# Hybrid encoder layer on one core: first loads on ScalarE's queue, weight sums issued behind attention rows, six tail residuals on TensorE

## The chip, the cores and the metric

The kernel runs on one core of one Trainium2 chip. The time is device microseconds of a whole execution, the median of several; lower is better. The core has five engines with a queue of instructions each, which a reader meets below under the names of the profile: PE (TensorE, matrix products), DVE (VectorE), ACT (ScalarE), POOL (GpSimd) and SP (SyncE, which here only issues DMAs). Every engine works through its own instructions in order. DMAs are issued by SP, ACT or POOL.

## The reference

One layer: a mixer (multi-scale causal pooling beside stick-breaking attention, gated and merged) and a squared-ReLU MLP, each between RMSNorms. 1024 tokens, width 1024, eight heads of 64, MLP width 4096, all in float32.

```python
h = rmsnorm(x, g_pre_mix)
proj = einsum('bsd,de->bse', h, w_in)            # [u_pool | q | k | v]
y_pool = multiscale_pool(u_pool, w_pool_mix, pool_scale) @ w_br_pool
o_sb = stick_breaking_attention(q, k, v)         # query blocks of 128, strictly causal
y_sb = o_sb @ w_br_sb
gates = sigmoid(h @ w_gate + b_gate)
merged = gates[..., :D] * y_pool + gates[..., D:] * y_sb
x = x + rmsnorm(merged @ w_out, g_post_mix)
h2 = rmsnorm(x, g_pre_mlp)
ff = square(relu(h2 @ w_up)) @ w_down
x = x + rmsnorm(ff, g_post_mlp)
```

## The kernel before

Everything is kept transposed: 128 channels on the partitions, tokens along the free axis, in two halves `h` of 512 tokens. To keep float32 precision, an operand is split into a rounded part `hi` (a copy on ACT) and a rest `lo` (a subtraction on DVE), and each product is three matmuls, hi·hi, lo·hi and hi·lo (`mm3`, L115 to L117). The MLP uses a seven-product scheme in place of eight block products, which is why sums of blocks of `w_down` are needed.

The order of instructions on each engine is set by a list scheduler when the kernel is built: code order gives the priority, `issue_after(i)` holds an instruction behind another, and whatever the scheduler takes to be ready may be moved ahead into an idle place of its engine's queue. On the chip a queue is then worked off strictly in that order.

Stages and names that matter here:

- `phase_in`: loads `x` and the weights `wraw` of the first projection `u` in pieces, splits them into `whi`/`wlo` (L295, L296) and `x` into `hT_hi`/`hT_lo` (L325, L326), and takes squares for the norm (L332, L334). `vt` holds all small vectors, `gn` is made of it. Nine matmuls on zeros (`idle`, L313) run before the first data is there.
- `phase_attention`: for each of 8 heads, eight rows of scores in the order 7 to 0 (`att_scores`: products `z`, sigmoids `F` and `T` on ACT, a mask on `T` by POOL's AFFINE_SELECT at L567, a scan and a product on DVE). Then `att_steps` transposes `T` on PE (`at`), splits it into `ahi`/`alo` and multiplies with `v` into `o` (L615). In one step of each group, POOL fills a part of `ahi` and `alo` with zeros (MEMSET, L596 and L597), and the product `o` of that step needs it. Gates (`dg`, `job_gate`) and the next head's q, k and v fill PE's queue between. A gate's result `gs` goes to DRAM as `gscr` by a POOL DMA (L521).
- `weight_sums`: a generator of 32 POOL DMAs in eight groups of four, each 1 MB from DRAM to DRAM (`wscr`). A sum starts as a plain copy (L1058) and gets a second block by an accumulating DMA (L1056). With `s1, s2, s3, s4 = self.wscr`, the groups are s3, s1 (copies), s3, s1 (accumulate), s2 from s3 (copy), s2 (accumulate), s4 from s2 (copy), s4 (accumulate). Before the change `job_gate` takes one step after each of the 32 `gscr` DMAs.
- `phase_post`: splits the attention output `oT` into `oh`, `ol` (L732, L733), multiplies with `w_br`, loads the gates back (`gate`), merges; then the output projection.
- `down`, `norm`, `last_tokens`: the last product is made for two quarters of 256 tokens; the last quarter's norm `r`, scaling (L1243), residual and output DMAs are the end of the program. Four of eight residuals there are added by PE with an identity matrix (`sums_pe`, L1233 and L1248) and copied out by ACT (L1249), the others by DVE (L1252).

Of the kernel before, what the change touches and what calls it, by code (L numbers as in the profile page):

```python
# [52 lines left out]
class Block:  # L53
# [118 lines left out]
    def build(self):  # L172
# [48 lines left out]
        nc.scalar.preload_act_table_set(TABLES)  # L221
# [29 lines left out]
    def phase_in(self):  # L251
# [24 lines left out]

        for g in range(3):
            load_w(nc.gpsimd, g, 0, 256)
        load(0, 0, 1)
        nc.sync.dma_start(self.vt, self.vec)  # L280
        nc.vector.tensor_scalar(out=self.gn, in0=self.vt[:, 0:32], scalar1=-0.5, scalar2=None, op0=ALU.mult)
        load(0, 1, 1)
        load_w(nc.sync, 0, 256, 512)
        load(0, 2, 1)
        load_w(nc.sync, 1, 256, 512)
        load_w(nc.sync, 2, 256, 512)
        load(0, 3, 1)
        load_w(nc.sync, 0, 512, 1024)
        load(0, 4, 2)
        load_w(nc.sync, 1, 512, 1024)  # L290
        load_w(nc.sync, 2, 512, 1024)
        load(0, 6, 2)
        for a, b in ((0, 256), (256, 512), (512, 1024)):
            for raw, hi, lo in us:
                nc.scalar.copy(hi[:, a:b], raw[:, a:b])  # L295
                nc.vector.tensor_sub(lo[:, a:b], raw[:, a:b], hi[:, a:b].bitcast(F32))  # L296
# [15 lines left out]
        for _ in range(9):  # L312
            nc.tensor.matmul(idle, zero[:, :P], zero, start=True, stop=True)  # L313
# [3 lines left out]
        for h in range(2):  # L317
            hi = self.big.tile([P, NK, H], F32R, name=f"hT_hi{h}", tag=f"big_hi{h}")
            lo = self.big.tile([P, NK, H], F32R, name=f"hT_lo{h}", tag=f"big_lo{h}")
            self.hT.append((hi, lo))  # L320
            acc = pa.tile([P, H], F32, name="acc", bufs=2)
            accs.append(acc)
            for k in range(NK):
                g = self.gn[:, k : k + 1]
                nc.scalar.activation(hi[:, k, :], xs[h][:, k, :], AF.Copy, scale=g)  # L325
                nc.vector.scalar_tensor_tensor(  # L326
                    out=lo[:, k, :], in0=xs[h][:, k, :], scalar=g, in1=hi[:, k, :].bitcast(F32),
                    op0=ALU.mult, op1=ALU.subtract,
                )
            for k in range(NK):  # L330
                sq = pa.tile([P, H], F32, name="sq", bufs=3) if k else acc
                nc.scalar.activation(sq, xs[h][:, k, :], AF.Square)  # L332
                if k:
                    nc.vector.tensor_add(acc, acc, sq)  # L334
# [179 lines left out]
    def job_gate(self, i, h):  # L514
        nc = self.nc
        d = self.dps.tile([P, H], F32, name="dg", tag="d")
        yield from self.dense_steps(d, self.weights(("g", i)), self.hT[h])
        s = self.sp.tile([P, H], F32, name="gs", tag="gs", bufs=2)
        nc.vector.tensor_mul(s, d, self.rb[h])
        self.after = nc.scalar.activation(s, s, AF.Sigmoid, bias=self.vt[:, V_BG + i : V_BG + i + 1])  # L520
        out = nc.gpsimd.dma_start(self.gscr[i][:, h * H : h * H + H], s)  # L521
        with self.tc.issue_after(out.ins):
            next(self.wsums)
# [16 lines left out]
    def att_scores(self, h, i):  # L540
# [13 lines left out]
        for c in range((w - 1) // H * H, -1, -H):  # L554
            n = min(H, w - c)
            top = c + n == w
# [9 lines left out]
            if top:  # L566
                nc.gpsimd.affine_select(  # L567
                    out=tl[:, w - P : w], in_=tl[:, w - P : w], pattern=[[-1, P]], compare_op=ALU.is_gt, fill=0.0,
                    base=0, channel_multiplier=1,
                )  # L570
# [74 lines left out]
    def phase_attention(self):  # L645
# [11 lines left out]
        for h in range(8):  # L657
# [9 lines left out]
            for n_row, i in enumerate(ROWS):  # L667
# [3 lines left out]
                self.pump(w_in * share[n_row])  # L671
                if h == 0 and n_row < 4:
# [50 lines left out]
    def phase_post(self):  # L723
# [3 lines left out]
        self.banks = 1  # L727
        oh, ol = [], []
        for p in range(4):
            oh.append(pp.tile([P, 1024], F32R, name=f"oh{p}"))  # L730
            ol.append(pp.tile([P, 1024], F32R, name=f"ol{p}"))
            nc.scalar.copy(oh[p], self.oT[p])  # L732
            nc.vector.tensor_sub(ol[p], self.oT[p], oh[p].bitcast(F32))  # L733
# [15 lines left out]
        def gated(e, b, ds):  # L749
# [18 lines left out]
        for e in range(8):  # L768
# [21 lines left out]
        for h in range(2):  # L790
# [270 lines left out]
    def down(self):  # L1061
# [152 lines left out]
        def norm(h, x1, gap, c=slice(0, H), behind=(None,), last_part=False):  # L1214
# [14 lines left out]
            n_pe = 4 if last_part else 0  # L1229
# [5 lines left out]
            for e in range(8):  # L1235
# [7 lines left out]
                nc.vector.scalar_tensor_tensor(  # L1243
                    out=t, in0=t, scalar=self.gn[:, V_POST_MLP + e : V_POST_MLP + e + 1], in1=r,
                    op0=ALU.mult, op1=ALU.mult,
                )
# [6 lines left out]
                (nc.sync if h == 1 or e % 2 or behind[0] else nc.scalar).dma_start(self.out[h, e][:, c], t)  # L1253

        def last_tokens(c, ops, side):

            n = c.stop - c.start
            squares = []
            for e in range(4):
# [10 lines left out]
                nc.scalar.activation(sq, f, AF.Square)  # L1270
                if e > 1:
# [91 lines left out]
```

## Time and profile before

| | |
|---|---|
| median of 3 runs | 1279.74 us (1278.86 to 1281.45) |
| profiled execution | 1278.63 us, of which the span of the profile is 1276.9 us |
| mean granted PE clock in it | 0.999 |
| PE busy | 1265.7 us, 99% |
| DVE, ACT, POOL busy | 925.7 us (72%), 611.0 us (48%), 172.1 us (13%) |
| DMA queues | 143.64 MB issued by SP, 88.49 MB by POOL |

Times inside the profile count from the start of the span. The timeline gives start, duration, engine, line and operation, and in brackets how long the engine was idle before it and what ended that. For DMAs the duration in the timeline is the issue; the time to landing is in the list of DMA issues. POOL's DMAs are the `wscr`, `gscr`, `gate`, `ascr` and `xscr` traffic.

### The profile page before, as it was taken

To read this page: it belongs to the slowest core of one execution; us is meant where nothing else is said; L and a number is where in the kernel's file an instruction comes from. 1 tells how busy PE (TensorE), PEld (TensorE's weight loads), DVE (VectorE), ACT (ScalarE), POOL (GpSimd) and SP (SyncE) were. 2 spreads that over 40 slices of the span, in tenths; PEclk is the share of its full clock that TensorE was granted. 3 is DMA by queue.
4 is the path that set the end of the run, shared out by engine and by line. 5 is a ranking of instruction groups with operands and counts; after the bars stand their busy time and mean duration, and the time that the engine had idled before them with its cause. 6 is when DMAs were issued, how large, how long until landed. Compare 5 with 4: busy or idle time off the path is not lost.

```text
span 1276.9 us, 16588 instructions
## 1 busy us (share of the span) xinstructions
PE 1265.7 (99%) x6035; PEld 1056.1 (83%) x6035; DVE 925.7 (72%) x1317; ACT 611.0 (48%) x1012; POOL 172.1 (13%) x314
## 2 busy tenths in 40 slices
PE   9999999999999999999999999999999999999997
PEld 6898888889888887888878888888888888888887
DVE  8787688787878737551777979877785655776975
ACT  8235455555555533132456646455454433344452
POOL 1002213211213230000101002211120000001000
PEclk9999999999999999999999999999999999999999
DMA  6254637742757997451529578655569546547651
GB/s 226 66 165 153 210 90 181 147 106 53 185 157 197 248 229 234 142 195 33 179 79 307 181 245 283 216 191 205 177 238 345 194 153 224 191 176 242 200 212 66
DMA packets 75745, 233.70 MB, mean 183 GB/s; under 512 B 8624, under 2 KB 11184, under 8 KB 73488
## 3 DMA queue, kind: packets, MB, share of 16 engines
q1 hardware_dynamic: 47936, 143.64, 34.4%
q0 software_dynamic: 27152, 88.49, 23.1%
q8 instruction: 47, 0.77, 0.2%
q10 hardware_dynamic: 576, 0.52, 0.1%
q14 instruction: 34, 0.28, 0.1%
HBM read 178.10 MB, written 83.89 MB: 205 GB/s over the span
## 4 chain that ended last, share of the span: by engine, by line
PE 91%; DVE 4%; issue 2%; ACT 1%; DMA 1%; POOL 0%; SPq 0%; DVEq 0%; ACTq 0%; POOLq 0%
PE d L116 20%; PE d L117 20%; PE d L115 20%; PE dg L117 4%; PE dg L116 4%; PE dg L113 4%; PE o L615 3%; PE at L590 2%; PE dqk L116 2%; PE dqk L117 2%; PE dqk L113 1%; PE z L563 1%; PE z L560 1%; PE du L116 1%; PE zu L116 1%
## 5 line engine op out<-in xcount | busy, mean ns | idle before, releaser
L116 PE MATMUL d<-blo,whi 128*128 128x512 f32 (+1 forms) x456 | 172.3, 378 | 0.0
L117 PE MATMUL d<-bhi,wlo 128*128 128x512 f32 (+1 forms) x456 | 171.9, 378 | 0.0
L115 PE MATMUL d<-bhi,whi 128*128 128x512 f32 (+1 forms) x456 | 168.7, 378 | 0.0
L573 DVE TENSOR_TENSOR_SCAN F<-F,past 128x512 f32<-128x512 f32 (+3 forms) x96 | 94.0, 979 | 22.4 <-ACT F L564 21.0
L85 ACT CAST whi<-wraw 128x512 fp32r<-128x512 f32 (+1 forms) x88 | 67.7, 800 | 72.4 <-PE d L116 35.0
L113 PE MATMUL dg<-hT_hi,whi 128*128 128x512 f32 x253 | 101.8, 402 | 0.0
L117 PE MATMUL dg<-hT_hi,wlo 128*128 128x512 f32 x256 | 100.8, 394 | 0.0
L116 PE MATMUL dg<-hT_lo,whi 128*128 128x512 f32 x256 | 100.4, 392 | 0.0
L86 DVE TENSOR_TENSOR wlo<-wraw,whi 128x512 fp32r<-128x512 f32 (+1 forms) x88 | 77.6, 904 | 30.1 <-ACT whi L85 30.0
L116 PEld LDWEIGHTS d<-blo,whi 128*128 128x128 f32 x456 | 85.7, 188 | 16.1
L117 PEld LDWEIGHTS d<-bhi,wlo 128*128 128x128 f32 x456 | 85.8, 188 | 15.9
L115 PEld LDWEIGHTS d<-bhi,whi 128*128 128x128 f32 x456 | 85.5, 188 | 15.8
L564 ACT ACTIVATE F<-z 128x512 f32<-128x512 f32 (+3 forms) x96 | 47.2, 493 | 61.6 <-DVE T L577 37.0
L116 PE MATMUL d<-b_lo,whi 128*128 128x512 f32 x196 | 76.2, 390 | 0.4 <-DVE b_lo L825 0.4
L115 PE MATMUL d<-b_hi,whi 128*128 128x512 f32 x196 | 75.6, 389 | 0.0
L117 PE MATMUL d<-b_hi,wlo 128*128 128x512 f32 x196 | 74.7, 389 | 0.0
L1112 DVE TENSOR_TENSOR wlo<-slots_hi,whi 128x1024 fp32r<-128x1024 f32 x29 | 35.5, 1225 | 52.3 <-ACT whi L1110 52.3
L599 DVE TENSOR_TENSOR alo<-at,ahi 128x512 fp32r<-128x512 f32 (+1 forms) x96 | 51.9, 553 | 24.8 <-ACT ahi L598 23.6
L1110 ACT CAST whi<-slots_hi 128x1024 fp32r<-128x1024 f32 x29 | 30.5, 1051 | 81.1 <-PE d L116 65.2
L598 ACT CAST ahi<-at 128x512 fp32r<-128x512 f32 (+1 forms) x96 | 45.1, 481 | 45.2 <-PE at L590 42.0
L1110 ACT CAST whi<-slots_lo 128x1024 fp32r<-128x1024 f32 x27 | 28.4, 1053 | 74.0 <-PE d L116 60.3
L577 DVE TENSOR_TENSOR T<-T,F 128x255 f32<-128x255 f32 (+4 forms) x96 | 52.8, 556 | 12.1 <-POOL T L567 4.2
(319 smaller groups left out, 3310.1 us busy)
## 6 DMA issues: line engine op xcount, KB each, us to landing
wraw<-w SPq DMA_DIRECT2D x80, 512.0 KB, 4.3
wscr<-w POOLq DMA_DIRECT2D x24, 1024.0 KB, 10.3
ext_b<-ascr SPq DMA_DIRECT2D x40, 512.0 KB, 4.3
gscr<-gs POOLq DMA_DIRECT2D x32, 256.0 KB, 4.8
gate<-gscr POOLq DMA_DIRECT2D x16, 512.0 KB, 3.7
pscr<-p SPq DMA_DIRECT2D x32, 256.0 KB, 3.2
braw<-w SPq DMA_DIRECT2D x16, 512.0 KB, 5.5
ascr<-c POOLq DMA_DIRECT2D x32, 256.0 KB, 4.7
```

The lines of the kernel that those rows point to most:

```text
L85: nc.scalar.copy(hi[:, c], raw[:, c])
L86: self.last_lo = nc.vector.tensor_sub(lo[:, c], raw[:, c], hi[:, c].bitcast(F32)).ins
L113: nc.tensor.matmul(ps, wh, rh, start=first and i == 0, stop=False)
L115: nc.tensor.matmul(ps, wh, rh, start=first and i == 0, stop=False)
L116: nc.tensor.matmul(ps, wh, rl, start=False, stop=False)
L117: nc.tensor.matmul(ps, wl, rh, start=False, stop=last and i == n - 1)
L564: nc.scalar.activation(f[:, c : c + n], z[:, :n], AF.Sigmoid, scale=-1.0)
L573: nc.vector.tensor_tensor_scan(fr, fr, past[:, c : c + n][:, ::-1], 1.0 if top else f[:, c + n : c + n + 1], ALU.mult, ALU.max)
L577: nc.vector.tensor_mul(tl[:, c:e], tl[:, c:e], f[:, c + 1 : e + 1])
L598: nc.scalar.copy(hi[:, c:], at[:, c:])
L599: nc.vector.tensor_sub(lo[:, c:], at[:, c:], hi[:, c:].bitcast(F32))
L1110: last_split[0] = nc.scalar.copy(hi, src).ins
```

## The change

**First loads.** `vt` and the first 256 columns of the three weights are issued by ACT, ahead of its table load; SP's pieces of weights are 256:640 and 640:1024, `x` comes in pieces of 1, 1, 1, 2 and 3 blocks. The splits of the weights are tied by `issue_after` between those of `x`, the squares run two blocks behind. One `idle` matmul fewer.

**Weight sums.** `job_gate` no longer takes a step. In the attention, a step is taken behind the mask of the second, fourth and seventh row of each head (24 steps); four more stand in `phase_post` and four in the output projection.

**Scores.** The row of 640 keys is cut into 384 + 256 columns and no longer into 512 + 256 (of which 128 were padding).

**Behind the attention.** In `phase_post` one `t` tile and one `ms` tile are allocated ahead of `oh`/`ol`, and the gating products are tied behind the last `ol`.

**Tail.** Six of the last eight residuals go to PE. In the last quarter the gain is multiplied in by ACT beforehand (`gain`), so that DVE's scaling is a plain product with `r`. The last two tiles go out on ACT's queue, the others on SP's.

```diff
-        nc.scalar.preload_act_table_set(TABLES)
...
+        nc.scalar.dma_start(self.vt, self.vec)
         for g in range(3):
-            load_w(nc.gpsimd, g, 0, 256)
+            issued = load_w(nc.scalar, g, 0, 256).ins
+        with tc.issue_after(issued):
+            nc.scalar.preload_act_table_set(TABLES)
...
+        for g in range(3):
+            load_w(nc.sync, g, 256, 640)
         load(0, 2, 1)
-        load_w(nc.sync, 1, 256, 512)
-        load_w(nc.sync, 2, 256, 512)
-        load(0, 3, 1)
...
+        load(0, 3, 2)
+        for g in range(3):
+            load_w(nc.sync, g, 640, 1024)
+        load(0, 5, 3)
...
-        for _ in range(9):
+        for _ in range(8):
             nc.tensor.matmul(idle, zero[:, :P], zero, start=True, stop=True)
...
+                if h == 0 and k in (0, 1, 3):
+                    split_w(*{0: (0, 256), 1: (256, 640), 3: (640, 1024)}[k])
...
-        out = nc.gpsimd.dma_start(self.gscr[i][:, h * H : h * H + H], s)
-        with self.tc.issue_after(out.ins):
-            next(self.wsums)
+        nc.gpsimd.dma_start(self.gscr[i][:, h * H : h * H + H], s)
...
-        for c in range((w - 1) // H * H, -1, -H):
-            n = min(H, w - c)
-            top = c + n == w
+        low = min(H, w - 2 * P) if w > H else 0
+        for c, n in ((low, w - low), (0, low)):
+            if n == 0:
+                continue
+            top = c == low
...
+                if n_row in (1, 3, 6):
+                    with tc.issue_after(self.masked.ins):
+                        next(self.wsums)
...
+        pp.tile([P, H], F32, name="t", tag="t0", bufs=2)
+        self.ps.tile([P, H], F32, name="ms", tag="ms", bufs=1)
...
-                nc.vector.tensor_mul(t, gt[:, h * H : h * H + H], ds[h])
+                with tc.issue_after(ol_done):
+                    nc.vector.tensor_mul(t, gt[:, h * H : h * H + H], ds[h])
...
+            if e % 2:
+                next(self.wsums)
...
+                if h == 0 and e % 2:
+                    next(self.wsums)
...
-            n_pe = 4 if last_part else 0
+            n_pe = 6 if last_part else 0
...
+                if last_part:
+                    nc.vector.tensor_mul(t, t, r)
+                else:
...
-                (nc.sync if h == 1 or e % 2 or behind[0] else nc.scalar).dma_start(self.out[h, e][:, c], t)
+                (nc.scalar if last_part and e >= n_pe else nc.sync).dma_start(self.out[h, e][:, c], t)
...
+                if side is not None:
+                    gain(4 + e)
+                    gain(e)
```

What the scheduler makes of it is seen in the order of each engine's instructions. In it `wscr_Q_122` to `125` are the four parts (Q = 0 to 3) of the sum s2, `wscr_Q_130` to `133` those of s4; `<-w` is the accumulating DMA, `<-wscr` the copy that starts a sum. s4 is copied from the finished s2 and then accumulates.

POOL before, in the sixth and seventh gate of the last heads: the four accumulations of s2 stand one behind each `gscr`, and the first copy of s4 follows four sums later.

```order
L521 DMA gscr_71<-gs 128x512
L1056 DMA wscr_1_123<-w 512x1x512
L596 MEMSET ahi 128x128
L597 MEMSET alo 128x128
L521 DMA gscr_79<-gs 128x512
L1056 DMA wscr_2_124<-w 512x1x512
L567 AFFINE_SELECT T<-T 128x128 x2
L521 DMA gscr_79<-gs 128x512
L1056 DMA wscr_3_125<-w 512x1x512
L567 AFFINE_SELECT T<-T 128x128
L521 DMA gscr_72<-gs 128x512
L1058 DMA wscr_0_130<-wscr_0_122 16x16384
```

Between the accumulation into a part of s2 and the copy that reads it, there are three other parts and several gates.

POOL now, from the seventh mask of the last head but one:

```order
L1091 DMA wscr_0_122<-w 512x1x512
L726 DMA yl_4856<-yscr_1_85 128x1024
L726 DMA yh_4858<-yscr_0_86 128x1024
L726 DMA yl_4860<-yscr_1_87 128x1024
L591 AFFINE_SELECT T<-T 128x128
L1093 DMA wscr_0_130<-wscr_0_122 16x16384
L544 DMA gscr_71<-gs 128x512
L1091 DMA wscr_0_130<-w 512x1x512
L620 MEMSET ahi 128x128
L621 MEMSET alo 128x128
L544 DMA gscr_79<-gs 128x512
L591 AFFINE_SELECT T<-T 128x128 x2
```

The scheduler has moved the eight steps that the code takes in `phase_post` and in the projection ahead into the last head. The copy into s4 now stands one mask behind the accumulation that it reads, and the next accumulation one `gscr` behind that copy.

POOL before, at the zero fill of the last head's first group (the third and fourth row), which stands directly behind the last mask:

```order
L567 AFFINE_SELECT T<-T 128x128
L596 MEMSET ahi 128x128
L597 MEMSET alo 128x128
L521 DMA gscr_73<-gs 128x512
L1056 DMA wscr_0_130<-w 512x1x512
L596 MEMSET ahi 128x128
```

POOL now, in the last head up to that same zero fill:

```order
L1093 DMA wscr_2_132<-wscr_2_124 16x16384
L591 AFFINE_SELECT T<-T 128x128
L544 DMA gscr_80<-gs 128x512
L1091 DMA wscr_2_132<-w 512x1x512
L591 AFFINE_SELECT T<-T 128x128
L1091 DMA wscr_3_125<-w 512x1x512
L544 DMA gscr_80<-gs 128x512
L726 DMA yh_4862<-yscr_0_88 128x1024
L726 DMA yl_4864<-yscr_1_89 128x1024
L591 AFFINE_SELECT T<-T 128x128
L1093 DMA wscr_3_133<-wscr_3_125 16x16384
L620 MEMSET ahi 128x128
```

The zero fill now stands behind the copy into the fourth part of s4, and that copy reads what the accumulation five rows above it writes.

ACT at the start, before:

```order
L221 ACT_TABLE_LOAD
L332 ACTIVATE acc<-x_179 128x512
L325 ACTIVATE hT_hi_250<-x_179,gn 128x512
L295 CAST whi<-wraw 128x256
L325 ACTIVATE hT_hi_250<-x_179,gn 128x512
L332 ACTIVATE sq<-x_179 128x512
L295 CAST whi<-wraw 128x256 x2
```

ACT at the start, now:

```order
L277 DMA vt<-vec 128x52
L274 DMA wraw<-w 128x256 x3
L281 ACT_TABLE_LOAD
L344 ACTIVATE hT_hi_230<-x_178,gn 128x512
L302 CAST whi<-wraw 128x256 x3
L344 ACTIVATE hT_hi_230<-x_178,gn 128x512
L302 CAST whi<-wraw 128x384 x3
```

The squares `acc` and `sq` (L332) have left the first rows, and the three first splits stand together.

ACT at the very end, before:

```order
L1249 COPY ff_0_8753<-d 128x256
L1253 DMA out<-ff_0_8753 128x256
L1249 COPY ff_1_8754<-d 128x256
L1249 COPY ff_2_8755<-d 128x256
L1249 COPY ff_3_8756<-d 128x256
L1253 DMA out<-ff_2_8755 128x256
```

ACT at the very end, now:

```order
L1287 COPY ff_3_8756<-d 128x256
L1287 COPY ff_4_8757<-d 128x256
L1291 DMA out<-ff_6_8759 128x256
L1287 COPY ff_5_8758<-d 128x256
L1291 DMA out<-ff_7_8760 128x256
```

Of the first six outputs none is on ACT's queue any more, and the output of `ff_6` stands ahead of the sixth copy.

More of the change, by code (lines that the diff above doesn't have):

```diff
@@ L322, in phase_in, with square @@
             accs.append(acc)
+            def square(k):
+                sq = pa.tile([P, H], F32, name="sq", bufs=3) if k else acc
+                with tc.issue_after(his[min(k + 2, NK - 1)]):
+                    nc.scalar.activation(sq, xs[h][:, k, :], AF.Square)
+                if k:
+                    with tc.issue_after(los[min(k + 2, NK - 1)]):
+                        nc.vector.tensor_add(acc, acc, sq)
+            his, los = [], []
             for k in range(NK):
                 g = self.gn[:, k : k + 1]
[L325 to L334, printed above, removed]
+                with after(turn[0]):
+                    his.append(nc.scalar.activation(hi[:, k, :], xs[h][:, k, :], AF.Copy, scale=g).ins)
+                with after(turn[1]):
+                    los.append(nc.vector.scalar_tensor_tensor(
+                        out=lo[:, k, :], in0=xs[h][:, k, :], scalar=g, in1=hi[:, k, :].bitcast(F32),
+                        op0=ALU.mult, op1=ALU.subtract,
+                    ).ins)
+                turn[:] = [his[-1], los[-1]] if h == 0 else [None, None]
+                if h == 0 and k in (0, 1, 3):
+                    split_w(*{0: (0, 256), 1: (256, 640), 3: (640, 1024)}[k])
+                if k > 1:
+                    square(k - 2)
+            turn[:] = [None, None]
+            square(NK - 2)
+            square(NK - 1)
         def stats(h):
@@ L732, in phase_post @@
             nc.scalar.copy(oh[p], self.oT[p])
[L733 removed]
+            ol_done = nc.vector.tensor_sub(ol[p], self.oT[p], oh[p].bitcast(F32)).ins
         mg = []
@@ L1242, in norm @@
                 t = ff[h][e][:, c]
[L1243 to L1246, printed above, removed]
+                if last_part:
+                    nc.vector.tensor_mul(t, t, r)
+                else:
+                    nc.vector.scalar_tensor_tensor(
+                        out=t, in0=t, scalar=self.gn[:, V_POST_MLP + e : V_POST_MLP + e + 1], in1=r,
+                        op0=ALU.mult, op1=ALU.mult,
+                    )
                 if e < n_pe:
```

25 lines of the change are left out of this document (13 added, 12 removed).

## The prediction

> **What bounds the kernel now.** The page's busy table comes first, then what PE waited for, then PE's rate in two stretches.
>
> ```profile
> span 1276.9 us, 16588 instructions
> PE 1265.7 (99%) x6035; PEld 1056.1 (83%) x6035; DVE 925.7 (72%) x1317; ACT 611.0 (48%) x1012; POOL 172.1 (13%) x314
> ```
>
> PE is busy 99% of the span. All its waits over the whole span, longest first (total, times, longest), are a few microseconds:
>
> ```profile
> PE idle L313 <- DVE zero L310: 1.4, 1, 1.4
> PE d L1248 <- DVE ff L1243: 1.2, 1, 1.2
> ...
> PE o L615 <- DVE alo L599: 0.2, 1, 0.2
> ```
>
> A modelled busy PE may hide slack, so the rate is counted too: matmuls in a stretch (first "x"), from the table of stretches.
>
> ```profile
> 5.69:9.46 3.77, 3.00 (x9) 1.60 (x10) 3.41 (x6) 2.98 (x6) 0.88 (x1) 1.00 0.98 349
> 900.00:1200.00 300.00, 300.00 (x1325) 248.37 (x1324) 204.55 (x222) 132.91 (x157) 19.42 (x36) 1.00 0.61 213
> ```
>
> Deep in the MLP 1325 matmuls of 512 columns take 300 us, 0.227 us each: that is PE's rate. So only four things can be gained: PE work itself, the start, the few waits, the tail. And anything that makes PE wait in the middle is paid in full, since PE has nothing to catch up with.
>
> **Start.** Rows of the first six microseconds:
>
> ```profile
> 1.42 4.02 PE L313 MATMUL idle<-zero 128*128 128x512 bf16 x9 [1.42 <-DVE zero L310]
> 1.24 0.42 SPq L280 DMA_DIRECT2D vt<-vec  x1
> 0.79 1.28 ACT L221 ACT_TABLE_LOAD   x1 [0.79 <-PEq L1354]
> 3.65 0.63 ACT L332 ACTIVATE acc<-x 128x512 f32<-128x512 f32 x1 [1.57 <-DMA x<-x]
> 3.84 0.22 DVE L281 TENSOR_SCALAR gn<-vt 128x32 f32<-128x32 f32 x1 [2.40 <-DMA vt<-vec]
> 4.18 0.71 ACT L325 ACTIVATE hT_hi<-x,gn 128x512 fp32r<-128x512 f32 x1
> 5.24 0.41 ACT L295 CAST whi<-wraw 128x256 fp32r<-128x256 f32 x1 [0.35 <-DMA wraw<-w]
> 5.70 0.50 PE L115 MATMUL du<-hT_hi,whi 128*128 128x512 f32 x1 [0.25 <-ACT whi L295]
> ```
>
> The first product starts at 5.70; nine matmuls then take 3.77 us where nine at rate take 2.04, so 1.73 us go on waits for splits. Now four issues at about 0.42 us stand on ACT ahead of its table load, which ends at 0.79 + 4 x 0.42 + 1.28 = 3.75: its cover is the landing of `x` (3.65), so it costs 0.1 at most. `hT_hi` follows at about 3.85 (0.33 earlier, without `acc` in front), and with the weights there, `whi` at 4.55 and PE at 5.0. That is 0.7. Eight `idle` matmuls end at 5.0; the ninth's loss costs nothing. The three splits in a row (0.4 each) then keep up with PE's 0.23 per product almost from the start, so I take 1.3 of the 1.73: 2.0 us in sum. Ends: all of it, 2.4, and a loss of 0.1 if the weights land no earlier.
>
> The Trainium skill, "DMA: Bandwidth & Descriptors", section "Issuing engines are not separate DMA queues", says that DMAs of all issuers interleave on the same 16 engines, so that another issuer saves only the time of issuing. By that rule I would count the earlier first product alone, 0.7 in place of 2.0, and the forecast would be 1.3 us higher; no run here shows the moved queue yet.
>
> **Scores.** Rows of PE around a product of 384 columns:
>
> ```profile
> 436.48 0.33 PE L560 MATMUL z<-k,q 128*128 128x384 f32 x1
> 436.65 0.34 PE L563 MATMUL z<-k,qs 128*128 128x384 f32 x1
> 436.82 0.40 PE L113 MATMUL dg<-hT_hi,whi 128*128 128x512 f32 x1
> ```
>
> A product of 384 starts 0.17 before the next one, one of 512 takes 0.227. The row of 640 keys has two such products per head: 16 x 0.055 = 0.9 us, all on PE's path. ACT and DVE handle the same columns as before.
>
> **Behind the attention.** The last `gscr`, its time to landing, and what follows:
>
> ```profile
> 474.94 0.57 POOL L521 DMA_DIRECT2D gscr<-gs  x1 [4.05 <-ACT gs L520]
> gscr<-gs POOLq DMA_DIRECT2D x1, 256.0 KB, 7.9
> 483.24 3.89 ACT L732 CAST oh<-oT 128x1024 fp32r<-128x1024 f32 x4 [7.29 <-issue]
> 483.65 0.39 PE L117 MATMUL d<-yh,wlo 128*128 128x512 f32 x1
> 485.94 0.39 PE L117 MATMUL d<-oh,wlo 128*128 128x512 f32 x1
> ```
>
> 474.94 + 7.9 = 482.9, and ACT's `oh` starts at 483.24: `oh` lies where `gs` lay and waits for its DMA. Four starts of PE from 483.65 to 485.94 take 2.29 us where three steps at rate take 0.68, so 1.6 us are lost. With `t` allocated first, `oh` no longer lies over `gs`, and `oT` was ready long before: 1.6 gained (ends 0 and 1.6). The tie of the gating products costs nothing, since DVE does `ol` first anyway and the banks give PE other products.
>
> **Weight sums.** This decides. The order of POOL shows that the scheduler has put all 32 sums into the attention, the last eight into the last head, where each copy into s4 reads an accumulation issued shortly before, and each accumulation into s4 reads that copy. Whether POOL then holds what is behind:
>
> ```profile
> 362.29 0.56 POOL L699 DMA_DIRECT2D yh<-yscr  x1 [4.29 <-DMA qs<-q]
> 399.62 0.47 POOL L567 TENSOR_SCALAR_AFFINE_SELECT T<-T 128x128 f32<-128x128 f32 x1 [2.30 <-ACT T L565]
> 453.58 0.21 POOL L596 MEMSET ahi<- 128x128 f32 x1 [3.45 <-issue]
> 455.20 1.25 POOL L1056 DMA_DIRECT2D wscr<-w  x1
> 455.69 0.28 PE L615 MATMUL o<-ahi,v 128*128 128x256 f32 x1
> ```
>
> The first row: POOL stood for 4.29 us because an issue waited for another DMA to land. The landings, as medians of the 16 accumulations and 8 copies, then of single ones (one alone; one with the next 3.9 us behind it; that next; one copy):
>
> ```profile
> wscr<-w POOLq DMA_DIRECT2D x16, 1024.0 KB, 10.7
> wscr<-wscr POOLq DMA_DIRECT2D x8, 6.8
> wscr<-w POOLq DMA_DIRECT2D x1, 1024.0 KB, 9.0
> wscr<-w POOLq DMA_DIRECT2D x1, 1024.0 KB, 11.0
> wscr<-w POOLq DMA_DIRECT2D x1, 1024.0 KB, 13.0
> wscr<-wscr POOLq DMA_DIRECT2D x1, 5.8
> ```
>
> On the clock of before, the chain starts with the accumulation behind the mask that ends at 400.1. It runs: landing; copy, landing; accumulation into s4 and the next one into s2 behind it; landing; and so on, four accumulations A and three copies C until the fourth copy is issued, and behind that the zero fill. Between a copy's landing and the next accumulation into s2, POOL spends 1.25 on the issue and 0.47 on a mask, the first time 1.46 more for two fills, a `gscr` and a mask: 3.2 + 1.7 + 1.7, and about 0.5 for the last copy. The fill comes at 400.1 + 7.1 + 4A + 3C. With the medians, 10.7 for the first A and 13.0 for the three that stand right behind another accumulation, and 6.8: 407.2 + 49.7 + 20.4 = 477.3, against 453.58 before. PE used the fill at 455.69, and two fills take 0.4, so it must come by 455.3: PE waits 22 us. With every landing the shortest seen, 9.0 and 5.8: 460.6, and PE waits 5.3. In between, the pair of 11.0 and 13.0 landed 13.0 + 3.9 - 11.0 = 5.9 apart, so an accumulation issued 3.2 or 1.7 behind one of 9.0 takes 11.7 or 13.2: 407.2 + 9.0 + 11.7 + 2 x 13.2 + 17.4 = 471.7, and PE waits 16 us. Masks are held as well, but inside the same delay. I take 18, between the last and the medians, as weight loads run beside the sums here too. What comes later (the eighth accumulation, a `gscr`, the fill of the last group) has 11 us of PE work in front of it and needs about 10, so it adds nothing.
>
> **Tail.** The end of the last quarter:
>
> ```profile
> 1265.95 0.42 ACT L1270 ACTIVATE sq<-ff 128x256 f32<-128x256 f32 x1 [0.92 <-DVE ff L1268]
> 1266.95 1.89 PE L1233 MATMUL d<-slots_hi,eye 128*128 128x256 f32 x8
> 1264.03 10.41 SPq L1253 DMA_DIRECT2D out<-ff  x9
> 1269.48 3.26 DVE L1243 SCALAR_TENSOR_TENSOR ff<-ff,gn,rb 128x256 f32<-128x256 f32 x8
> 1272.65 1.43 DVE L1252 TENSOR_TENSOR ff<-ff,slots_lo 128x256 f32<-128x256 f32 x4
> 1272.26 1.86 ACTq L1253 DMA_DIRECT2D out<-ff  x3
> ```
>
> The last output issue ends at 1274.44. Now DVE needs eight products at 0.36 to 0.41 and two sums at 0.36: `ff_6` is ready at 1272.7 to 1273.1. ACT issues it (0.4) ahead of the sixth copy (0.3), whose output SP then issues (0.42): 1273.85 to 1274.25. Gain 0.2 to 0.6, I take 0.4; an end of -0.2 if ACT's issue takes longer. The eight gains on ACT (0.42 each) and four more identity products (0.24 each) lie where ACT and PE idle.
>
> **Sum.** 1278.63 - 2.0 - 0.9 - 1.6 - 0.4 + 18 = 1291.7 us against the profiled execution, which lies 1.1 below the median of 1279.74; I say 1292.
>
> **Rivals.**
>
> 1. *POOL's waits stay hidden, the change is faster.* For it: no row of before shows a mask held by a sum, and all gains are independent of it. It holds if the landings fit in 455.3 - 407.2 = 48.1 us, that is, with copies of 5.8, if the four accumulations take under 7.7 each; the shortest was 9.0. Time: 1278.63 - 4.9 = 1273.7. Chance 0.15.
> 2. *All landings near their shortest.* A wait of 5.3 cancels the gains: 1279.0. Against it: the accumulations now stand in pairs, and the paired one took 13.0. Chance 0.07.
> 3. *PE's clock falls in the long waits.* The nine `idle` products took 4.02 us, 0.45 each, on a PE that had stood; at rate it is 0.227. If PE starts like that after two long waits, it loses 2 us each: 1296. Chance 0.16. The Trainium skill, "TensorE: Matmul & The Clock Gate", section "Why this matters for your kernels", says that PE gaps over about 3 us put the clock back to half; the row of the `idle` products agrees for the start, and no run here shows it in the middle.
>
> **How the numbers follow.** The forecast of a wait between 10 and 22 us has 0.62 and gives 1284 to 1296, its own range. With rival 3 the slower side has 0.78; rival 2 is no change, 0.07; rival 1 faster, 0.15. A run tells 0.2%, 2.6 us, from no change. The range 1278 to 1301 leaves out rival 1 and a few in a hundred above: its upper end is 22 us of wait with rival 3 and a start that gains little.
>
> **What would show it.** POOL waits of 6 to 13 us for landings of `wscr` between 395 and 495, four of each kind; PE waits before `o` at L639, the longest behind a fill by POOL; PE busy well under 80 in the 80 us there. The first `du` at 5.0 and no gap behind it; `oh` directly behind the table load; the last output issue about 0.4 earlier against the end of `r`. If masks and fills of the last head start on time, the forecast is wrong by its largest term.

## The result and the profile after

The changed kernel takes 1302.06 us (median of 4 runs, 1301.65 to 1304.34) against 1279.3 us for the kernel before: a ratio of 1.0179 with a 95% interval of 1.0167 to 1.0192, 22.8 us slower. The forecast was 1292 with a range of 1278 to 1301. The direction and the place were right; the time lies 1.1 us above the range. The profiled execution took 1302.0 us, its span 1300.3 us, 23.4 more than the span before.

The page of the changed kernel, busy table and the two rows of slices for PE and its granted clock:

```profile
span 1300.3 us, 16617 instructions
PE 1273.8 (98%) x6042; PEld 1063.0 (82%) x6042; DVE 924.5 (71%) x1315; ACT 615.0 (47%) x1022; POOL 166.4 (13%) x311
PE   9999999999999869999999999999999999999998
PEclk9999999999999989999999999999999999999999
```

Each slice is 32.5 us. Two slices (423 to 488 us, the last head of the attention) are not full, and in the same region the clock row drops. PE's busy time grew by 8.1 us although its products have as many columns as before (the scores lost 0.9 us of them, and eight more products with the identity matrix in the tail have the same again), so it was also slower while busy. What PE waited for, over the whole span (total, times, longest):

```profile
PE o L639 <- POOL ahi L620: 11.1, 2, 8.4
PE o L639 <- ACT ahi L622: 5.3, 2, 3.5
...
PE o L639 <- DVE alo L623: 0.8, 1, 0.8
```

These are 17.2 us, all before products `o` between 410 and 480 us, where the kernel before had 0.2 us. What POOL waited for between 380 and 500 us:

```profile
POOL wscr L1093 <- DMA wscr<-w: 36.9, 4, 11.0
POOL gscr L544 <- ACT gs L543: 19.0, 8, 6.2
POOL wscr L1091 <- DMA wscr<-wscr: 15.8, 3, 6.2
```

L1093 is the copy into s4, which waits for the accumulation into s2 (11.0 us at the longest); L1091 is the next accumulation, behind a wait for the copy. Three of these show and not four, since behind the second copy POOL stood for a gate until 438.28, and that copy landed at 438.75. Here are the four copies and the zero fill on POOL's timeline; the bracket gives the wait:

```profile
408.94 0.51 POOL L1093 DMA_DIRECT2D wscr<-wscr  x1 [6.93 <-DMA wscr<-w]
...
433.36 0.51 POOL L1093 DMA_DIRECT2D wscr<-wscr  x1 [8.08 <-DMA wscr<-w]
...
455.34 0.52 POOL L1093 DMA_DIRECT2D wscr<-wscr  x1 [11.04 <-DMA wscr<-w]
...
477.84 0.51 POOL L1093 DMA_DIRECT2D wscr<-wscr  x1 [10.81 <-DMA wscr<-w]
478.34 0.22 POOL L620 MEMSET ahi<- 128x128 f32 x1
```

The fill stands directly behind the last wait and comes at 478.34; before the change it came at 453.58. The products `o` that waited, on PE's timeline:

```profile
417.73 0.39 PE L639 MATMUL o<-ahi,v 128*128 128x256 f32 x1 [2.65 <-POOL ahi L620]
...
438.29 0.39 PE L639 MATMUL o<-ahi,v 128*128 128x256 f32 x1 [3.49 <-ACT ahi L622]
...
465.12 0.50 PE L639 MATMUL o<-ahi,v 128*128 128x512 f32 x1 [1.83 <-ACT ahi L622]
...
478.62 0.58 PE L639 MATMUL o<-ahi,v 128*128 128x256 f32 x1 [8.44 <-POOL ahi L620]
```

The second and third name ACT, but they too lead back to POOL: the split into `ahi` stood on ACT's queue behind a gate `gs`, and that gate's product on DVE's queue behind a `T` whose mask POOL issued late (the mask at 433.87 stands right behind the copy at 433.36, the one at 461.95 behind the accumulation at 461.27). And behind the long waits PE is slow. Stretches of 10 us; PE's busy time and count of products come first, the granted clock stands ahead of the last two columns:

```profile
420.00:430.00 10.00, 10.00 (x43) 8.06 (x43) 7.68 (x12) 6.42 (x14) 2.34 (x3) 0.87 1.11 209
...
440.00:450.00 10.00, 10.00 (x45) 8.21 (x44) 8.90 (x15) 5.63 (x12) 2.72 (x5) 0.85 0.97 190
...
460.00:470.00 10.00, 8.17 (x41) 6.48 (x39) 5.26 (x11) 3.29 (x8) 4.65 (x7) 1.00 0.77 155
470.00:480.00 10.00, 1.56 (x6) 1.19 (x5) 0.69 (x1) 0.59 (x1) 1.36 (x4) 0.69 1.25 350
480.00:490.00 10.00, 10.00 (x41) 8.24 (x40) 3.84 (x7) 3.43 (x7) 2.13 (x4) 0.80 0.53 105
```

After the waits of 2.65, 3.49 and 8.44 us the clock reads 0.87, 0.85 and 0.80, with PE busy all 10 us; after the wait of 1.83 it stays at 1.00.

**The account.** I sum the time from the start of each product to the start of the next, less 0.2266 us per 512 columns. Between 395 and 510 us that excess is 29.1 us, against 6.1 before and 4.5 in the kernel of the second experiment below, which has no such waits. The 24.5 us over that one are 19.1 in eight long steps (the waits) and 5.4 spread over short ones (the clock). The other differences of the two spans: start +0.6, a wait of 0.56 at 391 us (experiments 2, 3 and 5 have it too, so it does not come from the last eight sums), scores -0.9, the wait behind the attention -1.6, tail +0.2. Together 23.4.

The two parts do not simply add up in time. The product that the fill behind the fourth copy holds up is this one in experiment 2, which has the same order of products on PE, and this one in the kernel before:

```profile
456.90 0.36 PE L639 MATMUL o<-ahi,v 128*128 128x256 f32 x1
```
```profile
458.21 0.28 PE L615 MATMUL o<-ahi,v 128*128 128x256 f32 x1
```

In the changed kernel it starts at 478.62, 22.0 later than in experiment 2 when one counts in the 0.3 that the changed kernel was ahead at 380 us. Of these, 18.5 are standing and 3.5 slow products. But that fill hung on POOL's chain: each of the seven copies and accumulations from 408.94 to 477.84 that wait for the one before them was issued 0.3 to 0.5 us behind its landing, and only one mask between them waited for PE's side, 1.70 us for its `T`. So the slow products ahead of the fill mostly came out of the wait for it, and the clock made the kernel longer by little more than what was lost behind the fill, 2.5 us. This is worked out from the rows; no run has these waits with PE at full rate.

The start, ACT, DVE and PE:

```profile
4.66 0.18 DVE L282 TENSOR_SCALAR gn<-vt 128x32 f32<-128x32 f32 x1 [2.84 <-DMA vt<-vec]
4.88 0.72 ACT L344 ACTIVATE hT_hi<-x,gn 128x512 fp32r<-128x512 f32 x1 [0.91 <-DVE gn L282]
...
5.61 0.40 ACT L302 CAST whi<-wraw 128x256 fp32r<-128x256 f32 x1
...
6.07 0.80 PE L115 MATMUL du<-hT_hi,whi 128*128 128x512 f32 x1 [1.05 <-ACT whi L302]
...
7.51 0.63 PE L116 MATMUL du<-hT_lo,whi 128*128 128x512 f32 x1
...
7.94 0.63 PE L116 MATMUL zu<-hT_lo,whi 128*128 128x512 f32 x1
```

`vt` now lands so late that `gn` starts at 4.66 (3.84 before), the first product at 6.07 (5.70 before), and then products are 0.43 apart until about 9.2. The first weights came no earlier either: issued by ACT at 1.24 they landed at 5.59, just ahead of their split, and issued by POOL at 1.32 they had landed at 5.22. The loads of `x` and `vt` issued at 0.80, after (with sizes and time to landing):

```profile
x<-x SPq DMA_DIRECT2D x1, 256.0 KB, 3.7
vt<-vec ACTq DMA_DIRECT2D x1, 26.0 KB, 3.8
```

Before, both issued by SP (at 0.80 and 1.24):

```profile
x<-x SPq DMA_DIRECT2D x1, 256.0 KB, 2.8
...
vt<-vec SPq DMA_DIRECT2D x1, 26.0 KB, 2.6
```

The tail, DVE and the two queues, and the last issue with its time to landing; `r` ends at 1292.67 here:

```profile
1292.70 2.77 DVE L1279 TENSOR_TENSOR ff<-ff,rb 128x256 f32<-128x256 f32 x8
1295.39 0.75 DVE L1290 TENSOR_TENSOR ff<-ff,slots_lo 128x256 f32<-128x256 f32 x2
```
```profile
1287.24 9.86 SPq L1291 DMA_DIRECT2D out<-ff  x11
```
```profile
out<-ff SPq DMA_DIRECT2D x1, 128.0 KB, 2.3
```

The last issue ends 4.43 us behind `r`, where it was 4.99 before; but the last landing takes 2.3 us instead of 1.9, and the program ends 7.63 behind `r` where it was 7.45.

### The profile page after: what moved, and what is told of

It is laid out like the page before. It is cut to its first block, busy times and chain, and to the rows that moved or that the text cites. A ratio compares the mean times of both kernels' runs of the same rounds, so it can differ in the third digit from the quotient of the medians.

```text
span 1300.3 us, 16617 instructions
## 1 busy us (share of the span) xinstructions
PE 1273.8 (98%) x6042; PEld 1063.0 (82%) x6042; DVE 924.5 (71%) x1315; ACT 615.0 (47%) x1022; POOL 166.4 (13%) x311
## 4 chain that ended last, share of the span: by engine, by line
PE 87%; DMA 5%; DVE 3%; issue 2%; ACT 1%; POOL 1%; ACTq 0%; DVEq 0%; POOLq 0%
PE d L116 20%; PE d L117 20%; PE d L115 20%; DMA wscr<-w 4%; PE dg L117 3%; PE dg L116 3%; PE dg L113 3%; PE o L639 2%; PE dqk L117 2%; PE dqk L116 2%; PE at L614 2%; PE dqk L113 1%; PE dv L117 1%; PE dv L116 1%; PE z L587 1%
## 5 line engine op out<-in xcount | busy, mean ns | idle before, releaser
L597 DVE TENSOR_TENSOR_SCAN F<-F,past 128x256 f32<-128x256 f32 (+2 forms) x96 | 94.1, 980 | 19.4 <-ACT F L588 18.4
L588 ACT ACTIVATE F<-z 128x256 f32<-128x256 f32 (+2 forms) x96 | 47.2, 493 | 69.7 <-DVE T L601 49.7
L601 DVE TENSOR_TENSOR T<-T,F 128x255 f32<-128x255 f32 (+3 forms) x96 | 53.1, 556 | 34.8 <-POOL T L591 27.0
```

The costliest lines, as they stand in the source:

```text
L588: nc.scalar.activation(f[:, c : c + n], z[:, :n], AF.Sigmoid, scale=-1.0)
L597: nc.vector.tensor_tensor_scan(fr, fr, past[:, c : c + n][:, ::-1], 1.0 if top else f[:, c + n : c + n + 1], ALU.mult, ALU.max)
L601: nc.vector.tensor_mul(tl[:, c:e], tl[:, c:e], f[:, c + 1 : e + 1])
```

## The experiments

The measured time of the kernel before in each session is given with each result.

**1. Sums at the gates again, all else as changed.**

```diff
-                if n_row in (1, 3, 6):
-                    with tc.issue_after(self.masked.ins):
-                        next(self.wsums)
...
-        nc.gpsimd.dma_start(self.gscr[i][:, h * H : h * H + H], s)
+        out = nc.gpsimd.dma_start(self.gscr[i][:, h * H : h * H + H], s)
+        with self.tc.issue_after(out.ins):
+            next(self.wsums)
```

> The changed kernel with the weight sums stepped by the gates again, everything else as changed. Counted from the trace of the changed kernel (time between starts of products, less 0.2266 us per 512 columns): waits before `o` 19.1 us, slow products behind them 5.3 us more than before, start 0.6 later, tail 0.2 longer, scores 0.9 shorter, the wait behind the attention 1.5 shorter. If the sums carry all of 24.4 us: 1279.3 + 0.6 + 0.2 - 0.9 - 1.5 = 1277.7. By the prediction's terms for the other edits (4.9 gained): 1274.4. Rival: the slow products are not caused by the waits, then 5 us of them stay: 1283. The PE clock stays at 1.00 over the whole attention if the first holds.

Measured: 1277.58 us, before 1278.91, ratio 0.9985 (0.9975 to 0.9994); mean clock 1.00, no wait before `o` between 395 and 510 us. The sums carry the whole loss, and the slow products went with the waits. All other edits together gain 1.3 us, not 4.9.

**2. Only the last eight sums held.** The copies into s4 are tied between the gate loads of the post stage, the accumulations behind the last of them; POOL issues both, so the tie holds its queue order.

```diff
+            self.loaded = nc.gpsimd.dma_start(gt, self.gscr[i]).ins
...
             if e % 2:
-                next(self.wsums)
+                with tc.issue_after(self.loaded):
+                    next(self.wsums)
```

(and the same tie in the output projection)

> The changed kernel with its last eight sums tied behind gate loads on POOL's queue (four copies between the gate loads, four accumulations behind the last), so that they leave the last head; the other 24 stay behind the masks. If the chain of copy and accumulation in the last head is the cause: no wait of POOL for wscr in the attention, 1277.7 like the kernel with sums at the gates. Rival: any sum behind a mask holds the masks, whatever it reads; then the waits before `o` are nearly the same and the time stays above 1295. Second rival: the sums now load the DMA engines beside the gate loads and the post stage pays some us: 1280 or more.

Measured: 1277.75 us, before 1278.91, ratio 0.9990 (0.9981 to 1.0000). The 24 sums that still stand behind masks cost nothing that the times show (0.2 us over experiment 1): it is the copy behind its own accumulation that holds POOL. In the post stage the load of the sums is hidden.

**3. The same, with 12 idle products.**

```diff
-        for _ in range(8):
+        for _ in range(12):
             nc.tensor.matmul(idle, zero[:, :P], zero, start=True, stop=True)
```

> The kernel with the last eight sums held, and 12 idle products at the start in place of 8, so that PE has no gap of 1.05 us before the first product at 6.07. Eight products there start 0.43 apart in the changed kernel and not 0.227. If that is PE's clock, lost in the gap or never reached: the products are 0.23 apart except where splits are late, 1.5 to 2 us off the kernel with 8, so 1276. Rival: the products are slow since weights and splits land late, whatever the clock: within 0.3 of the kernel with 8.

Measured: 1277.37 us, before 1278.91, ratio 0.9989 (0.9980 to 0.9999); 0.4 below the kernel with 8, too little to tell from none by ten runs of each, so the trace has to decide. The stretch from the first product to 10.5 us, in the changed kernel and here:

```profile
6.06:10.50 4.44, 4.37 (x11) 3.17 (x12) 3.65 (x9) 3.61 (x8) 0.00 (x0) 1.00 0.92 265
```
```profile
6.18:10.50 4.32, 4.26 (x18) 2.99 (x17) 3.58 (x8) 3.40 (x8) 0.00 (x0) 1.00 0.96 276
```

18 products in place of 11, with splits no earlier: the products of 0.43 us were PE's speed, not late data. (The clock column reads 1.00 in both; here the count of products tells it, not the column.) The expectation of 1.5 to 2 us still missed: of the 1.3 us gained in the first 20 us, 0.7 went into a new wait at 41 us, where PE needs a bank that DVE frees.

**4. The kernel before with only the sums moved.**

```diff
-        with self.tc.issue_after(out.ins):
-            next(self.wsums)
...
+                if n_row in (1, 3, 6):
+                    with tc.issue_after(self.masked.ins):
+                        next(self.wsums)
```

(and the eight steps in the post stage and the projection, as in the change)

> The kernel before with only the sums moved as in the change (behind masks, eight steps behind the attention). If the sums alone make the loss: 1279.3 + 24.4 = 1303.7, with POOL waits of 5 to 11 us for wscr in the last head and the clock below 1 behind each wait of PE over 2.5 us. If the waits cost what the prediction took and the clock nothing: 1297. Rival: other edits (scores, start) share in the loss by moving masks against sums: under 1295.

Measured: 1302.01 us, before 1278.91, ratio 1.0177 (1.0160 to 1.0194): the whole loss. The profile, of an execution of 1304.81 us, shows the same two groups of waits, PE's and POOL's:

```profile
PE o L613 <- POOL ahi L594: 9.8, 2, 5.6
```
```profile
POOL wscr L1063 <- DMA wscr<-w: 37.5, 4, 11.0
POOL wscr L1061 <- DMA wscr<-wscr: 20.3, 3, 8.2
```

The product behind that same fill starts at 481.16, 22.9 later than in the kernel before, nearly as in the changed kernel, though the parts differ: 17.3 standing and 5.7 slow products. More slow products ahead of the fill, and less standing for it.

**5. The last eight sums held, with the start of before** (its loads, splits, squares and nine idle products; the diff is that part of the change undone).

> The kernel with the last eight sums held (1277.75) and the first loads, splits, squares and nine idle products as they were before the change. Counted from the traces, the start of before is 0.6 us shorter than the changed one. And at the end of the program SP looks at its DMA semaphores in a fixed order, 0.06 us each: in the changed kernel the last output's semaphore is the second of eight, so that six looks follow the last landing; with the start of before two DMAs fewer stand on the hardware queues, the semaphores go round by two, and the last output's is the last looked at: 0.37 us less. So 1276.8. Rival, the order of the looks is without effect: 1277.15. Rival, the prediction's gain of 2.0 at the start was real and is only hidden: 1279.7.

Measured: 1276.78 us, before 1279.32, ratio 0.9976 (0.9967 to 0.9984), the fastest kernel of the study. Against experiment 2 that is 1.0 less, but the two ran in different sessions, and the kernel before was 0.4 slower in this one. The traces tell what it is: counted by the starts of products, the work of the first 20 us is done 0.9 sooner here, so the changed start is a loss, and the end is 0.36 shorter. The program ends 0.91 us behind the last landing, in all kernels with the changed start 1.27. The records of SP's looks at the DMA semaphores show why: they follow each other 0.06 us apart in a fixed order; in the changed kernel seven looks come from 1299.04 to 1299.41, after the last landing at 1299.02, and in the kernel before only one, at 1276.02.

**6. The last eight sums held, `vt` back on SP.**

```diff
-        nc.scalar.dma_start(self.vt, self.vec)
...
         load(0, 0, 1)
+        nc.sync.dma_start(self.vt, self.vec)
```

> The kernel with the last eight sums held, with the vector `vt` loaded by SP behind the first block of x as before the change; the first weights stay on ACT's queue. If `vt` lands late because it stands on ACT's queue, the first hT_hi starts at 3.9 to 4.1 instead of 4.8 and then the weights decide: they were waited for until 5.24 before the change when POOL issued them. If another issuer does not make them land earlier, the first product starts at 5.5 to 5.7 and its products still take 0.43 each: 1277.4 to 1277.8. Rival, the prediction's picture: weights there by 4.5, first product at 5.0, full rate, 1276 or less.

Measured: 1277.34 us, before 1279.32, ratio 0.9982 (0.9973 to 0.9991). The time is as expected, the reason is not. The first hT_hi starts at 4.77, not at 3.9, since both still land late:

```profile
x<-x SPq DMA_DIRECT2D x1, 256.0 KB, 3.4
vt<-vec SPq DMA_DIRECT2D x1, 26.0 KB, 3.3
```

So it is not ACT's queue that delays `vt`. What is left of the difference to before in the first two microseconds is that the first weights are issued from 0.80 on beside the first block of `x`, and by POOL from 1.32 on before: more transfers run at once, and the two that everything waits for land 0.5 to 0.7 later. That this crowd is the cause is argued; no run moves only the time at which the weights are issued.

**7. Only the last four sums held**: the copies into s4 stay in the last head, each behind its accumulation; the accumulations into s4 are tied behind the last gate load. The diff is that of experiment 2 without the tie in the post stage.

> The changed kernel with only its last four sums (the accumulations into s4) held until behind the gate loads; the four copies into s4 still stand in the last head, each behind the accumulation into s2 that it reads. If the waits of POOL add up along the chain, what is left is four landings of 9.6 and some 7 us of other work, 45 us, less than the 55 that PE allows: the fill comes in time and the time is 1277.8, though POOL waits 3 to 9 us four times. Rival, each wait of POOL behind a mask costs PE something by itself: the time is a good half of the loss, 1285 to 1292, with PE waits before `o`.

Measured: 1278.98 us, before 1279.32, ratio 0.9991 (0.9982 to 1.0001). Between 395 and 480 us POOL waited

```profile
POOL wscr L1094 <- DMA wscr<-w: 17.6, 3, 7.3
```

and PE, between 380 and 520 us,

```profile
PE o L639 <- POOL ahi L620: 0.9, 1, 0.9
```

POOL stood 17.6 us for sums and PE paid 0.9 for it, 1.1 by the excess between 395 and 510 us (5.7 against 4.5 in experiment 2). The time is 1.2 above what was expected, since the fill came just too late and not in time. The waits add up along the chain, and PE pays only what goes beyond its slack: against experiment 2 its products fall back at that one place. The rival, that each wait costs something by itself, would have given 1285 to 1292 and is out.

**8. Stands of known length.** The kernel before with a program behind its last output: bursts of 36 products of 512 columns, parted by chains of DVE work (its time says nothing here).

```diff
+        def burst(n):
+            d = self.bank()
+            for _ in range(n):
+                nc.tensor.matmul(d, q[:, 0:P], z[:, 0:H], start=True, stop=True)
+            return d
...
+        for widths in ([], [P], [256], [H], [H, P], [H] * 2, [H] * 3, [H] * 4, [H] * 5, [H] * 6, [H] * 8, [H] * 12, [H] * 20):
+            gap(burst(36), widths)
+        for n in (2, 4, 6, 7, 8, 9, 10, 12):
+            gap(burst(36), [H] * 20)
+            gap(burst(n), [256])
```

> The kernel before with a program added behind its last output: bursts of 36 products of 512 columns, parted by chains of DVE work of growing length (PE stands 0.5 to 10 us), and then bursts of 2 to 12 products after a long stand, a gap of about 1 us, and 36 products more. Theory from the traces so far: a stand of 2.0 us costs nothing, one of 2.9 or more makes the products after it take 0.43 each for about 3 us, some 1.5 us lost, and the loss grows little with the stand. For the start: 8 products and a gap of 1 us leave the next ones slow for 3 us or more, 9 products and a short gap do not. Rival: the loss grows with the stand in proportion (2.4 us were lost after 8.7). Rival for the start: the slow products there come from late splits, and after a gap of 1 us the products here run at 0.23.

PE's timeline; the second column is the length of a burst of 36, the bracket the stand ahead of it:

```profile
1345.54 8.44 PE L1332 MATMUL d<-whi 128*128 128x512 f32 x36 [2.12 <-DVE whi L1339]
1356.56 10.03 PE L1332 MATMUL d<-whi 128*128 128x512 f32 x36 [2.58 <-DVE whi L1339]
1369.63 8.42 PE L1332 MATMUL d<-whi 128*128 128x512 f32 x36 [3.04 <-DVE whi L1339]
1381.56 10.04 PE L1332 MATMUL d<-whi 128*128 128x512 f32 x36 [3.50 <-DVE whi L1339]
1396.03 11.33 PE L1332 MATMUL d<-whi 128*128 128x512 f32 x36 [4.43 <-DVE whi L1339]
...
1434.67 10.82 PE L1332 MATMUL d<-whi 128*128 128x512 f32 x36 [9.97 <-DVE whi L1339]
...
1531.84 10.04 PE L1332 MATMUL d<-whi 128*128 128x512 f32 x36 [1.07 <-DVE whi L1339]
...
1556.66 8.45 PE L1332 MATMUL d<-whi 128*128 128x512 f32 x36 [1.06 <-DVE whi L1339]
```

8.44 us is full rate. All stands up to 2.12 us cost nothing, one of 2.58 cost 1.6, one of 3.04 nothing, those from 3.50 up 1.6 to 2.9, and 9.97 less than 4.43: the loss does not grow in proportion. The last two rows follow a stand of 9.96, then 7 and 8 products and a gap of 1.06: after 7 the next burst was slow, after 8 it was not. So a gap of 1 us alone costs nothing; what matters is how long PE had worked ahead of it: 3.33 us (7 products) were too few, 3.75 (8) were enough, though these 8 themselves still ran at half rate. In the changed kernel 8 idle products and a gap of 1.05 were not enough, so 8 lies at the edge. Each of these stands was measured once.

**9. The last eight sums held, loads as before, splits and squares in the changed order, ten idle products** (the diff is the undone loads, and 10 in place of 8).

> The kernel with the last eight sums held and the first loads issued as before the change (vectors on SP, first weights on POOL, table load first), but with the changed order of the splits (three weight splits together, squares two blocks behind) and ten idle products, which end at 5.7, when the first product of before started. If the changed start lost by its loads and by PE's clock and its order of splits is good in itself: PE at full rate from the first product, no gap from late squares, some 0.5 us below the kernel with the whole start of before (1276.8), so 1276.3. Rival: with all three weights needed at once their landings (5.2 to 7.8 before the change) set the products, and the order of the splits gains nothing: 1276.8 or more.

Measured: 1280.86 us, before 1279.05, ratio 1.0007 (0.9997 to 1.0016); the expectation missed by 4.6. The first 20 us are 0.7 shorter than in experiment 5, as hoped. But at 44 us PE stands, and then is slow (the row of PE, then the stretch behind it):

```profile
44.36 0.54 PE L115 MATMUL du<-hT_hi,whi 128*128 128x512 f32 x1 [2.91 <-DVE u L413]
```
```profile
44.40:48.60 4.20, 4.20 (x12) 3.33 (x13) 4.20 (x9) 0.00 (x0) 0.00 (x0) 0.59 0.36 125
```

Twelve products in 4.2 us, clock 0.59. DVE's `u` needs the norm of `x`, whose last step ends at 42.48 here and at 40.84 in experiment 5; here a split `wlo` of 1.22 us then goes ahead of `u` on DVE, so that `u` starts 2.8 later. The norm begins with the product `ms` of the squares, which with the late squares stands 17 products later on PE (37.89 here, 34.71 in experiment 5). Time won at the start was given back with interest at the first place where PE needs that chain.

## Why the prediction was wrong, point by point

The sum said 1291.7 and the profiled execution took 1302.0. The 10.3 us between are 4.0 of the delay up to the fill at 478.34, 2.5 of the clock behind it, 2.6 of the start, 0.6 of the tail and 0.6 of the wait at 391 us. The upper end of the range had room for 26 us of waits and clock, and 24.5 came: it was passed because the start and the tail, put in as gains, were losses, and by the wait at 391 us.

- **Weight sums, +18: the mechanism was right, the term too small by 4.0; this is the step that failed most.** The copies waited for accumulations to land four times, the accumulations for copies three times, and the fill behind the last copy came late. It came at 478.34, where the row of medians had given 477.3 and my middle value 471.7; the 18 that I took stands for 473.3. The first accumulation and the three paired ones took 9.6, 12.2, 14.6 and 15.1 us to land, not 9.0, 11.7, 13.2 and 13.2, and the mask that waited for its `T` cost 1.7. The delay at the product behind the fill was 22.0, not 18. A misreading kept it from being more: I took the product at 455.69 for the one that needs the fill, but that one ran at 469.34 in the changed kernel, ahead of the fill; the next of 256 columns needs it, so PE had about 1 us more than I gave it. That is luck.
- **The clock, 0 in the sum: the second step that failed, 2.5.** I put it aside as rival 3 with a chance of 0.16 and a price of 4 (two waits of 2 us). The slow products took 5.4, behind three waits, but 3.5 of them lie ahead of the fill, inside the delay of 22.0. The row for it, idle products at 0.45 each, was in the profile of before. The Trainium skill, "TensorE: Matmul & The Clock Gate", section "Why this matters for your kernels", has the rule of PE gaps over about 3 us. The changed kernel agrees for 3.49 and 8.44 us, which lost speed, and for 1.83, which did not; but 2.65 lost speed too, and in experiment 8 2.58 lost and 3.04 did not, so by the measurements there is no sharp edge. The same page of the Trainium skill, section "What's actually happening", says that the clock goes by a free-running window. That would explain this disorder; no run here tests it. Forecasting waits of 10 to 22 us in one head, I should have had this in the main line.
- **Start, -2.0: wrong in sign, +0.6.** I took the landing of `x` from before (3.65) and assumed that weights issued earlier land earlier without cost to others. `x` and `vt` landed 0.8 later instead (experiment 6: not by ACT's queue; that it was the crowd is argued), and the first weights 0.4 later. And the ninth idle product was not free: with 8 and a gap of 1.05 us, the next seven products ran at half rate (experiment 3). The rule that I weighed there, from the Trainium skill, "DMA: Bandwidth & Descriptors", "Issuing engines are not separate DMA queues", says that all DMAs interleave on the same engines, which fits. I drew from it only that the weights would not come earlier (0.7 gained instead of 2.0), not that the other loads would come later.
- **Scores, -0.9:** that is the work left out; no run moves it alone, but the account closes with it.
- **Behind the attention, -1.6: right.** The excess from 395 to 510 us fell from 6.1 to 4.5 in experiment 2, and no wait of PE for `oh` is left.
- **Tail, -0.4: wrong, +0.2.** The last issue came 0.56 earlier, as said (0.2 to 0.6). But the last landing came only 0.2 earlier: before the change the last five outputs had landed 0.36 to 0.40 us apart, which points to the transfers as the limit, not the issues. Then 0.37 was lost in SP's last looks. The identity products added are eight, not four as I wrote; they lie where PE idles.
- **Sum by the account:** 1278.6 + 0.6 - 0.9 - 1.6 + 0.2 + 19.1 + 5.4 = 1301.4, and 0.6 for the wait at 391 us gives the 1302.0 of the profiled execution.

The version that beats both is experiment 5: the scores, the order behind the attention and the tail of the change, with the start of before and the last eight sums tied behind gate loads, 1276.78 us.

## What to carry to other kernels

A DMA that reads what a DMA issued just ahead of it writes holds its whole in-order queue for the landing; ask what else stands in that queue, and add such waits up along the chain against the slack of the engine that needs it, since up to the slack they cost nothing (17.6 us of POOL's waiting cost 0.9) and beyond it everything. A step meant for later must be tied to an instruction of the same queue, or the scheduler takes it early. Where a forecast has the matrix engine stand for more than about 2.5 us, add about 2 us for its clock behind the last of such stands; slow products ahead of a wait whose end another engine's chain sets are hidden in that wait. And time saved at a start counts only up to the next place where another engine's chain is late.

## What the runs showed of the hardware that I had not expected

- The clock's loss jumps: 0 for stands up to 2.12 us, 1.6 at 2.58, 0 at 3.04, 1.6 at 3.50, 2.9 at 4.43, 2.4 at 9.97, in a burst of 8.44 us, each seen once.
- A load of 26 KB issued first of all on ACT's queue, at 0.80, took 3.8 us to land and came at 4.64; issued at 1.24 behind another on SP's queue it had taken 2.6 us and come at 3.82. On SP's queue, but beside the same loads of weights (experiment 6), it took 3.3 us.
- The end of a program costs 0.06 us for each DMA semaphore that is looked at after the last landing: 0.37 us for an output whose semaphore stood early in the order.
